# Memory rows and six of sixteen weight pieces loaded into the residual's two row places, and the first weight splits ordered behind the last block of the stage before

## The chip, the cores and the metric

The program runs on one core of a Trainium2 chip. A core has a matrix engine (PE, the trace also names its weight loads PEld), two engines for elementwise work (DVE and ACT), a third slower one (POOL), and SP, which here only issues transfers. The metric is the device time of one execution in microseconds, taken as the median of several runs. Lower is better.

## The reference, cut to what matters

One decoder layer over 1024 tokens of width 1024 in float32: a latent attention and a retention in parallel, one output projection, a cross-attention to 256 memory tokens, and a mixture of 32 gated MLPs. The change lies where the first two meet the third:

```python
x = x + jnp.concatenate([a_out, r_out], axis=-1) @ w_out[l]
hc = rms_norm(x, cross_norm_g[l])
m = rms_norm(mem, mem_norm_g[l])
# memory_cross_attention(hc, m, ...):
q = rms_norm((h @ w_q).reshape(B, S, CROSS_HEADS, CROSS_HEAD_DIM), q_qk_g)
kv = m @ w_kv                       # (256 x 1024) @ (1024 x 2048)
k = rms_norm(kv[..., :D_MODEL].reshape(B, M, CROSS_HEADS, CROSS_HEAD_DIM), k_qk_g)
v = kv[..., D_MODEL:].reshape(B, M, CROSS_HEADS, CROSS_HEAD_DIM)
```

## The kernel before, in words

**Products in three parts.** Every float32 factor is split into a high part (ACT rounds it, `wh`, `oTH`, `mTH`) and a low part (DVE subtracts, `wl`, `oTL`, `mTL`). A product is three matmuls: high by high, high by low, low by high (`mm3`). `split` makes the two parts.

**Weights.** `wpiece` loads two row blocks of a weight matrix (two transfers of 256 KB) into one `raw` place of 512 KB, and splits each block, with the norm's gain multiplied in. `raw` has three places (`RB = 3`), the split pieces have seven (`WB = 7`). `wchunk` makes the four pieces of a column chunk of 512. A `raw` place comes free when both low parts are taken; a split place when the matmuls that read it are done.

**Stages around the change.** Stage C is the latent attention in eight blocks of 128 tokens, with the output projection `out_part` of each block behind it. `out_part(7)`, the last one, needs the transposed attention output `oa` as `oTH` and `oTL`, runs 24 matmuls into `ps_sc`, adds the residual (`xa`, DVE) and squares the sum (ACT, tile names `ps_sc<-xa`). Stage E0 loads the memory rows in two tiles of 128 tokens (512 KB each), takes their squares (ACT, `ckn,sqm<-...`), scales them (DVE) and transposes them on PE into `mTH` and `mTL`. Stage E1 multiplies them with `cross_w_kv`: four column chunks, each with two memory tiles and eight row blocks, 192 matmuls of 128x512 in all. I number the sixteen weight pieces p0 to p15; chunk c uses p(4c) to p(4c+3). Then come the eight pieces of `cross_w_q` (wq0 to wq7) through the same three `raw` places, the first residual rows (`load_x1`, tiles `x1` with two places of 512 KB), their transposes (`x1TH`, `x1TL`), and stage E, the cross-attention. `load_down(0)` also issues one 1 MB load of an expert's weights early in E1.

**What sets the order.** A list scheduler places instructions engine by engine from priorities (`PRI`, `self.at`) and its own costs. At run time each engine executes its list strictly in order; SP likewise issues its transfers in order, and a transfer that has to wait holds up all behind it.

**Before the change**, the two memory tiles took two of the three `raw` places from stage C until PE had transposed them; the first pieces of `cross_w_kv` went through the third place one after the other, and p0 to p2 were split in the middle of stage C.

Of the kernel before, what the change touches and what calls it, by code (L numbers as in the profile page):

```python
# [24 lines left out]
F32 = mybir.dt.float32  # L25
# [4 lines left out]
AF = mybir.ActivationFunctionType  # L30
# [6 lines left out]
D = 1024  # L37
# [68 lines left out]
class Layer:  # L106
    def __init__(self, tc, a, out, dbg=None, stop=None):
        self.tc, self.nc, self.a, self.out, self.dbg, self.stop = tc, tc.nc, a, out, dbg or {}, stop
        self.banks, self.alias, self.place = {}, {}, [1, 2, 3, 4]
        self.ob, self.aT = 1, None  # L110


    def slot(self, shape, dtype=F32, name="t", bufs=2, pool=None, tag=None):
# [36 lines left out]
    def split(self, H, L, src, scale=None):  # L150

        nc = self.nc
        if scale is None:
            nc.scalar.activation(H, src, AF.Copy)  # L154
            return nc.vector.tensor_tensor(L, src, H.bitcast(F32), OP.subtract)
        else:
            self.high = nc.scalar.activation(H, src, AF.Copy, scale=scale)  # L157
            return nc.vector.scalar_tensor_tensor(L, src, scale, H.bitcast(F32), OP.mult, OP.subtract)  # L158

    def transposes(self, dst, src, n):  # L160
# [6 lines left out]
        e = self.mhalf[:, :1].to_broadcast(sh) if len(sh) == 2 else self.mhalf[:, :1, None].to_broadcast(sh)  # L167
        self.nc.gpsimd.tensor_tensor(out, v, e, OP.pow)

    def wpiece(self, srcs, n, gains, name):  # L170

        raw = self.wtile().rearrange("p (k n) -> p k n", k=2)
        pool, bufs = self.W
        if bufs:
            H, L = [pool.tile([128, 2, 512], F32R, name="w" + x, tag="w" + x, bufs=bufs) for x in "hl"]
        else:

            t = pool.tile([128, 2, 2, 512], F32R, name="w", tag="dn%d" % self.place.pop(0), bufs=1)
            H, L = t[:, 0], t[:, 1]
        for i, s in enumerate(srcs):  # L180
            dst = raw[:, i, :n]
            if len(s.shape) == 3:
                dst = dst.rearrange("p (g c) -> p g c", g=s.shape[1])
            self.nc.sync.dma_start(dst, s)
        if gains is None:
            self.split(H[:, :len(srcs), :n], L[:, :len(srcs), :n], raw[:, :len(srcs), :n])
        else:
            for i in range(len(srcs)):
                self.split(H[:, i, :n], L[:, i, :n], raw[:, i, :n], gains[i])
        return [(H[:, i, :n], L[:, i, :n]) for i in range(len(srcs))]  # L190

    def wchunk(self, w, n, gain, nk=8):

        r = []
        for k in range(0, nk, 2):
            ks = [k, k + 1] if k + 1 < nk else [k]
            r += self.wpiece([w(i) for i in ks], n, None if gain is None else [gain[i] if isinstance(gain, list) else gain[:, i:i + 1] for i in ks], "w")
        return r

    def project(self, out, xt, w, part=slice(None)):  # L200
# [585 lines left out]
    def out_part(self, tb, w, ret, role):  # L786

        nc = self.nc
        rows = slice(tb * 128, (tb + 1) * 128)
        if ret is None and tb >= 6:  # L790
            oT = self.split_T(self.oa[tb].rearrange("p h c -> p (h c)"), 4, "oT", self.ob, self.O)
        else:
            m = self.slot([128, 512], name="mr", bufs=self.ob, pool=self.O)
        if ret is not None:
            nc.sync.dma_start(m, ret[rows, :])
            oT = self.to_T(m, 4, "oT", self.ob, role, self.O)
        elif tb < 6:
            nc.sync.dma_start(m.rearrange("v (h t) -> v h t", h=NH),
                              self.mad.rearrange("(h v) t -> v h t", h=NH)[:, :, rows])
            oT = self.split_T(m, 4, "oT", self.ob, self.O)  # L800
        for c in range(2):
            cols = slice(c * 512, (c + 1) * 512)
            xr = self.slot([128, 512], F32, "xr", 1, self.O) if ret is not None else self.slot([128, 512], F32, "xa", XA)
            nc.sync.dma_start(xr, self.a["x"][0][rows, cols] if ret is not None else self.x1d[rows, cols])
            p = self.bank(role)
            self.project(p, oT, w[c])
            nc.vector.tensor_tensor(xr, p, xr, OP.add)
            nc.sync.dma_start(self.x1d[rows, cols], xr)
            if ret is None:
                self.square(self.sx1[:, tb, c:c + 1], xr, p)  # L810
                if "x1" in self.dbg:
                    nc.sync.dma_start(self.dbg["x1"][rows, cols], xr)
# [9 lines left out]
    def phase_e0(self):  # L822

        nc, a, sm = self.nc, self.a, self.sm
        gg = []
        for name in ("cross_q_qk_g", "cross_k_qk_g"):
            g = self.small([128, 2], "g_" + name, bufs=1)
            nc.sync.dma_start(g, a[name][0].rearrange("(k p) -> p k", p=128))
            gg.append(g)
        ggc = sm.tile([128, 2], F32, name="ggc", bufs=1)  # L830
        nc.vector.tensor_tensor(ggc, gg[0], gg[1], OP.mult)
        self.mT = []
        for m in range(2):
            mt = self.wtile("mem")
            nc.sync.dma_start(mt, a["mem"][0][m * 128:(m + 1) * 128, :])
            sq = self.small([128, 4], "sqm")
            for i in range(2):
                self.square(sq[:, i:i + 1], mt[:, i * 512:(i + 1) * 512], self.slot([128, 512], name="ckn", pool=self.CK))
            nc.vector.tensor_tensor(sq[:, 2:3], sq[:, 0:1], sq[:, 1:2], OP.add)
            self.inv_rms(sq[:, 3:4], sq[:, 2:3], D, "rm")  # L840
            self.scaled("mt", mt, mt, sq[:, 3:4])
            self.mT.append(self.to_T(mt, 8, "mT", 4, pool=self.E0))
        self.ggc = ggc

    def phase_e1(self):
        nc, a, mT, ggc = self.nc, self.a, self.mT, self.ggc
        w = a["cross_w_kv"][0]
        self.cK = [[self.slot([128, 2, 256], F32R, "cK", 8, self.KV) for _ in range(2)] for _ in range(NH)]
        self.cV = [[None, None] for _ in range(2)]
        for c in range(4):  # L850
            wc = self.wchunk(lambda k: w[k * 128:(k + 1) * 128, c * 512:(c + 1) * 512], 512, self.gain["mem_norm_g"])
            for m in range(2):
                p = self.bank("pj")
                self.project(p, mT[m], wc)
                if c >= 2:
                    v = [self.slot([128, 512], F32R, "cV" + s, 4, self.KV) for s in "HL"]
                    self.split(*v, p)
                    self.cV[m][c - 2] = v
                    continue
                ph = p.rearrange("p (h c) -> p h c", h=2)  # L860
                st = self.small([128, 2], "stk")
                for h in range(2):
                    self.square(st[:, h:h + 1], ph[:, h], self.slot([128, 256], BF, "jm", 1, self.CK))
                f = self.small([128, 2], "fk")
                self.inv_rms(f, st, 256, "fk")
                kn = self.slot([128, 2, 256], name="ckn", pool=self.CK)
                nc.vector.tensor_tensor(kn, ph, f[:, :, None].to_broadcast([128, 2, 256]), OP.mult)
                with self.at("e1t"):
                    tr = self.bank("tr")
                    self.transposes(tr, kn.rearrange("p h c -> p (h c)"), 4)  # L870
                    for i in range(4):
                        h, d = 2 * c + i // 2, i % 2
                        ms = slice(m * 128, (m + 1) * 128)
                        self.split(self.cK[h][0][:, d, ms], self.cK[h][1][:, d, ms], tr[:, i * 128:(i + 1) * 128],
                                   ggc[:, d:d + 1])
# [826 lines left out]
```

## Time and profile before

| What | Value |
|---|---|
| median of 3 runs | 1211.96 us (1209.45 to 1214.25) |
| the profiled execution | 1214.96 us, of which the span shown is 1213.2 us |
| PE busy | 1162.8 us, 96% of the span |
| DVE, ACT busy | 771.3 us, 652.3 us |
| stages C to E1, roughly | 290 to 530 us, then 530 to 585 us |

All positions are microseconds from the start of the span. A row of the timeline gives start, duration, engine, line, instruction, its output and inputs; in brackets stands the idle time of that engine just before it, and who ended it. Matmul durations overlap: the distance between starts is what a matmul costs (about 0.23 us for 128x512 at full clock). PEclk is the share of full clock that the chip granted: 1.0 is 2.4 GHz, 0.5 is 1.2 GHz.

### The profile page before, as it was taken

The page shows a single profiled execution, that of the slowest core. Times are in us where ns is not written, and L with a number is a line of the kernel's source. Part 1 is how long each engine was busy: PE and PEld are TensorE (multiplying, and loading weights), DVE is VectorE, ACT ScalarE, POOL GpSimd, SP SyncE. Part 2 cuts the span into 40 slices and gives each one's busy share as a digit, 9 for nine tenths or more (in the row PEclk, how much of TensorE's full clock was granted, in tenths as well). Part 3 has the DMA queues.
Part 4 walks back from the last instruction along what each step waited for, and adds up shares of the span by engine and source line. Part 5 has one row for each costly group of instructions (what it writes and reads, how often), then busy time and mean ns, then how long its engine had stood idle before and what let it go on. Part 6 is the DMA issues. An engine that isn't in the chain of part 4 may idle for free. (4 is left out here: it accounts for less than half of the span.)

```text
span 1213.2 us, 18340 instructions
## 1 busy us (share of the span) xinstructions
PE 1162.8 (96%) x6325; PEld 910.7 (75%) x6325; DVE 771.3 (64%) x1938; ACT 652.3 (54%) x1508; POOL 152.0 (13%) x152
## 2 busy tenths in 40 slices
PE   8999999998999999989999999999699999999995
PEld 7887878776688888878899998778565655566552
DVE  5646464678675786658644445555677777777672
ACT  8723232446554664557644446322477777777672
POOL 1011010121100000000000000000222222222222
PEclk9999999999999999999999999999799999999998
DMA  7622020204323433276611024985799999999982
GB/s 237 181 58 80 11 76 10 89 21 132 100 87 104 153 96 120 81 243 191 218 62 62 27 62 150 314 287 210 263 343 343 342 337 334 315 317 315 320 294 45
DMA packets 115472, 213.23 MB, mean 176 GB/s; under 512 B 20577, under 2 KB 68705, under 8 KB 107185
## 3 DMA queue, kind: packets, MB, share of 16 engines
q1 hardware_dynamic: 106912, 194.59, 47.0%
q0 software_dynamic: 7280, 17.37, 6.2%
q8 instruction: 51, 0.84, 0.3%
q14 instruction: 45, 0.36, 0.1%
q10 hardware_dynamic: 1184, 0.07, 0.1%
HBM read 179.69 MB, written 40.11 MB: 181 GB/s over the span
## 5 line engine op out<-in xcount | busy, mean ns | idle before, releaser
L145 PE MATMUL ps_pj<-wh,xT 128*128 128x512 f32 (+1 forms) x640 | 219.9, 403 | 1.8 <-ACT wh L157 1.2
L158 DVE SCALAR_TENSOR_TENSOR L<-raw,g,H 128x512 fp32r<-128x512 f32 x256 | 180.4, 748 | 55.1 <-ACT H L157 52.2
L157 ACT ACTIVATE H<-raw,g 128x512 fp32r<-128x512 f32 x256 | 169.5, 713 | 32.1 <-PE ps_pj L145 22.7
L145 PEld LDWEIGHTS ps_pj<-wh,xT 128*128 128x128 f32 x640 | 121.1, 190 | 21.1 <-ACT wh L157 1.6
L145 PE MATMUL ps_pj<-wl,xT 128*128 128x512 f32 (+1 forms) x320 | 127.9, 400 | 0.0
L1500 PE MATMUL ps_sc<-raw,aT 128*96 128x512 f32 x256 | 117.6, 602 | 1.2 <-ACT aT L1484 1.0
L145 PE MATMUL ps_pj<-H,xH 128*96 128x512 f32 x256 | 116.2, 454 | 0.0
L145 PE MATMUL ps_pj<-L,xH 128*96 128x512 f32 x256 | 102.6, 401 | 0.1
L145 PE MATMUL ps_pj<-H,xL 128*96 128x512 f32 x256 | 102.0, 398 | 0.0
L1500 PEld LDWEIGHTS ps_sc<-raw,aT 128*96 128x96 f32 x256 | 39.1, 162 | 65.1 <-issue 51.1
L1492 POOL DMA_INDIRECT out_dram<-y,idx x31 | 54.4, 1756 | 201.4 <-ACT H L157 161.6
L145 PE MATMUL ps_pj<-x1TH,wh 128*128 128x256 f32 x256 | 74.3, 290 | 2.6 <-ACT x1TH L154 2.6
L145 PE MATMUL ps_pj<-x1TL,wh 128*128 128x256 f32 x256 | 75.2, 294 | 0.0
L145 PE MATMUL ps_pj<-x1TH,wl 128*128 128x256 f32 x256 | 74.4, 291 | 0.0
L145 PEld LDWEIGHTS ps_pj<-wl,xT 128*128 128x128 f32 x320 | 61.1, 191 | 8.5 <-DVE wl L158 0.5
L145 PEld LDWEIGHTS ps_pj<-H,xH 128*96 128x96 f32 x256 | 42.5, 166 | 22.3 <-issue 7.5
L459 ACT ACTIVATE tg<-ps_pj,rh 128x128 f32<-128x128 f32 x32 | 11.7, 366 | 87.7 <-PE ps_pj L145 87.6
L145 PEld LDWEIGHTS ps_pj<-L,xH 128*96 128x96 f32 x256 | 41.7, 163 | 22.4 <-DVE L L158 8.6
L145 PEld LDWEIGHTS ps_pj<-H,xL 128*96 128x96 f32 x256 | 41.5, 162 | 16.0 <-issue 0.7
L145 PEld LDWEIGHTS ps_pj<-x1TH,wh 128*128 128x128 f32 x256 | 48.4, 189 | 3.0 <-ACT x1TH L154 3.0
L1030 ACT ACTIVATE cP<-ps_sc,cnb,fcq 128x256 f32<-128x256 f32 x32 | 17.8, 561 | 57.9 <-DVE cnb L1025 57.9
L145 PEld LDWEIGHTS ps_pj<-x1TH,wl 128*128 128x128 f32 x256 | 48.6, 190 | 0.0
(412 smaller groups left out, 2882.3 us busy)
## 6 DMA issues: line engine op xcount, KB each, us to landing
raw<-in_expert_w_down_dram SPq DMA_DIRECT2D x32, 1024.0 KB
raw<-in_expert_w_gate_dram SPq DMA_DIRECT2D x32, 1024.0 KB
raw<-in_expert_w_up_dram SPq DMA_DIRECT2D x32, 1024.0 KB
raw<-in_w_in_dram SPq DMA_DIRECT2D x32, 256.0 KB
raw<-in_cross_w_kv_dram SPq DMA_DIRECT2D x32, 256.0 KB
x<-x1d SPq DMA_DIRECT2D x16, 512.0 KB
xr<-in_x_dram SPq DMA_DIRECT2D x16, 256.0 KB
raw<-in_w_out_dram SPq DMA_DIRECT2D x16, 256.0 KB
```

Of the source, the lines that this page charges most:

```text
L145: mm = lambda s, m, i, e: self.nc.tensor.matmul(out, s, m, start=i, stop=e, skip_group_check=skip)
L157: self.high = nc.scalar.activation(H, src, AF.Copy, scale=scale)
L158: return nc.vector.scalar_tensor_tensor(L, src, scale, H.bitcast(F32), OP.mult, OP.subtract)
L459: nc.scalar.activation(tg, p[:, 384:512], AF.Tanh, scale=rh[:, tb:tb + 1])
L1030: nc.scalar.activation(P[:, js], s[:, js], AF.Exp, bias=nb[:, j:j + 1], scale=f[:, j:j + 1], accum_out=su[:, j:j + 1])
L1492: add = lambda c, cs: sums.append(nc.gpsimd.indirect_dma_start(out=out, out_offset=bass.IndirectOffsetOnAxis(ap=rows[:, c:c + 1], axis=0), ...
L1500: nc.tensor.matmul(py[:CAP], act[:, j * CAP:(j + 1) * CAP], wd[:, j, cs], start=(j == 0), stop=(j == 1))
```

## The change

It has three parts. The memory tiles are loaded into the two `x1` places. Pieces 1, 3, 6, 8, 11 and 13 of `cross_w_kv` are loaded into the `x1` places too, the other ten into `raw`. The high parts of the first chunk's pieces are ordered, for the scheduler, behind the high part of the last block's `oT` (`self.last`); the wait is one of order alone, with no semaphore of its own.

```diff
     def split(self, H, L, src, scale=None):
         if scale is None:
-            nc.scalar.activation(H, src, AF.Copy)
+            self.high = nc.scalar.activation(H, src, AF.Copy)
             return nc.vector.tensor_tensor(L, src, H.bitcast(F32), OP.subtract)
         else:
             self.high = nc.scalar.activation(H, src, AF.Copy, scale=scale)
+            if self.first:
+                self.after(self.high, self.first, "rows of the stage before first")
...
-    def wpiece(self, srcs, n, gains, name):
+    def wpiece(self, srcs, n, gains, name, raw=None):
-        raw = self.wtile().rearrange("p (k n) -> p k n", k=2)
+        raw = (self.wtile() if raw is None else raw).rearrange("p (k n) -> p k n", k=2)
...
     def out_part(self, tb, w, ret, role):
             oT = self.split_T(self.oa[tb].rearrange("p h c -> p (h c)"), 4, "oT", self.ob, self.O)
+            self.last = self.high
...
     def phase_e0(self):
-            mt = self.wtile("mem")
+            mt = self.slot([128, D], F32, "x1", 2, self.X1)
...
     def phase_e1(self):
+        raw = lambda i: self.slot([128, D], F32, "x1", 2, self.X1) if i % 5 in (1, 3) else None
         for c in range(4):
-            wc = self.wchunk(lambda k: w[k * 128:(k + 1) * 128, c * 512:(c + 1) * 512], 512, self.gain["mem_norm_g"])
+            self.first = None if c else self.last
+            wc = self.wchunk(lambda k: w[k * 128:(k + 1) * 128, c * 512:(c + 1) * 512], 512, self.gain["mem_norm_g"],
+                             raw=lambda i: raw(4 * c + i))
```

Three places in the lists show what moves. First ACT at the end of stage C, before the change; `mem_6104` and `mem_6134` are the memory tiles, `oTH_6027` is the last block's transposed output, `wh_6200` are the high parts of p3 and `wh_6307` those of p4:

```order
L731 ACTIVATE oa_5942<-ps_po_5824 128x512
L348 ACTIVATE ckn_6107,sqm_6106<-mem_6104 128x512
L348 ACTIVATE ckn_6109,sqm_6106<-mem_6104 128x512
L348 ACTIVATE ckn_6137,sqm_6136<-mem_6134 128x512
L348 ACTIVATE ps_sc_5993,sx1_3381<-xa_5991 128x512
L348 ACTIVATE ckn_6139,sqm_6136<-mem_6134 128x512
L154 ACTIVATE oTH_6027<-oa_5942 128x512
L348 ACTIVATE ps_sc_6011,sx1_3381<-xa_6009 128x512
L157 ACTIVATE wh_6200<-raw_6199,mem_norm_g_351 128x512 x2
L348 ACTIVATE ps_sc_6033,sx1_3381<-xa_6031 128x512
L348 ACTIVATE ps_sc_6051,sx1_3381<-xa_6049 128x512
L157 ACTIVATE wh_6307<-raw_6306,mem_norm_g_351 128x512
```

The same place after the change, where the memory tiles are `x1_6104` and `x1_6134` and `wh_6173` are the high parts of p0:

```order
L734 ACTIVATE oa_5942<-ps_po_5824 128x512
L351 ACTIVATE ps_sc_5993,sx1_3381<-xa_5991 128x512
L351 ACTIVATE ckn_6107,sqm_6106<-x1_6104 128x512
L351 ACTIVATE ckn_6109,sqm_6106<-x1_6104 128x512
L351 ACTIVATE ps_sc_6011,sx1_3381<-xa_6009 128x512
L154 ACTIVATE oTH_6027<-oa_5942 128x512
L157 ACTIVATE wh_6173<-raw_6172,mem_norm_g_351 128x512 x2
L351 ACTIVATE ckn_6137,sqm_6136<-x1_6134 128x512
L351 ACTIVATE ckn_6139,sqm_6136<-x1_6134 128x512
L351 ACTIVATE ps_sc_6033,sx1_3381<-xa_6031 128x512
L351 ACTIVATE ps_sc_6051,sx1_3381<-xa_6049 128x512
L154 ACTIVATE mTH_6121<-ps_tr_6116 128x512
```

`oTH_6027` now stands behind the second square of the residual (`ps_sc_6011`), and `mTH_6121` directly behind the last one, with no weight split between. Second, SP's list at the same place, before the change (`raw_6306` is p4, `raw_6315` p5, `raw_6808` the expert's 1 MB):

```order
L888 DMA x1_6630<-x1d_60 128x1024
L808 DMA x1d_60<-xa_6009 128x512
L804 DMA xa_6031<-x1d_60 128x512
L804 DMA xa_6049<-x1d_60 128x512
L184 DMA raw_6306<-in_cross_w_kv_dram 128x512
L808 DMA x1d_60<-xa_6031 128x512
L184 DMA raw_6306<-in_cross_w_kv_dram 128x512
L808 DMA x1d_60<-xa_6049 128x512
L184 DMA raw_6315<-in_cross_w_kv_dram 128x512 x2
L1411 DMA raw_6808<-in_expert_w_down_dram 128x2x1024
L184 DMA raw_6324<-in_cross_w_kv_dram 128x512 x2
```

And after it (`x1_6181` is p1, `x1_6199` p3, `x1_6324` p6; p0, p2 and p4 are issued in stage C, before these rows):

```order
L839 DMA x1_6134<-in_mem_dram 128x1024
L812 DMA x1d_60<-xa_6009 128x512
L808 DMA xa_6031<-x1d_60 128x512
L808 DMA xa_6049<-x1d_60 128x512
L186 DMA raw_6315<-in_cross_w_kv_dram 128x512 x2
L812 DMA x1d_60<-xa_6031 128x512
L812 DMA x1d_60<-xa_6049 128x512
L186 DMA x1_6181<-in_cross_w_kv_dram 128x512 x2
L1419 DMA raw_6808<-in_expert_w_down_dram 128x2x1024
L186 DMA x1_6199<-in_cross_w_kv_dram 128x512 x2
L186 DMA x1_6324<-in_cross_w_kv_dram 128x512 x2
```

The second memory tile stands where the second residual tile was loaded, p1 behind the last write of the residual, and p3 behind the 1 MB load. The residual rows themselves are now loaded between the last pieces of `cross_w_kv` and the first of `cross_w_q`. On PE the matmuls of chunk 0 are the same 48, but those of the two memory tiles alternate, where before the first tile's 24 stood ahead of the second's.

## Rows read from the trace of the kernel before

**Rows 1.** The page: busy share of each engine over the span.
```profile
PE 1162.8 (96%) x6325; PEld 910.7 (75%) x6325; DVE 771.3 (64%) x1938; ACT 652.3 (54%) x1508; POOL 152.0 (13%) x152
```
**Rows 2.** Timeline of PE, lines with a wait, and two starts beside them.
```profile
524.74 0.50 PE L145 MATMUL ps_sc<-wh,oTH 128*128 128x512 f32 x1 [0.61 <-ACT oTH L154]
...
530.32 1.03 PE L162 MATMUL ps_tr<-ident,mem 128*128 128x128 f32 x8
533.75 0.50 PE L145 MATMUL ps_pj<-wh,mTH 128*128 128x512 f32 x1 [2.40 <-ACT mTH L154]
...
547.89 0.60 PE L162 MATMUL ps_tr<-ident,ckn 128*128 128x128 f32 x4
...
586.93 0.58 PE L145 MATMUL ps_pj<-x1TH,wh 128*128 128x256 f32 x1 [2.59 <-ACT x1TH L154]
```
**Rows 3.** Windows: length, busy time (instructions) of PE, PEld, DVE, ACT, POOL, PEclk, DMA share, GB/s.
```profile
440.00:460.00 20.00, 20.00 (x112) 17.02 (x112) 15.27 (x38) 12.52 (x35) 1.01 (x1) 1.00 0.60 190
...
535.00:540.00 5.00, 5.00 (x20) 4.21 (x19) 3.57 (x6) 2.42 (x4) 0.00 (x0) 0.66 0.93 306
540.00:584.00 44.00, 44.00 (x203) 35.37 (x201) 32.27 (x61) 31.42 (x69) 2.80 (x4) 1.00 0.65 209
584.00:590.00 6.00, 3.41 (x16) 2.95 (x15) 4.21 (x8) 4.15 (x8) 0.00 (x0) 0.72 0.49 159
236.00:240.00 4.00, 2.48 (x13) 1.72 (x12) 2.29 (x9) 1.09 (x5) 1.02 (x1) 1.00 0.23 82
```
**Rows 4.** Timeline of PE: the longest wait inside the window 236 to 240.
```profile
238.40 0.33 PE L162 MATMUL ps_trp<-ident,kn 128*128 128x128 f32 x1 [1.52 <-DVE kn L608]
```
**Rows 5.** Tile `raw`, 400 to 525 us: duration min/median/max, first and last start.
```profile
L157 ACT ACTIVATE wh<-raw,mem_norm_g x6: 710/726/739, 436.8 to 453.1; 128x512 fp32r<-128x512 f32 x6
L158 DVE SCALAR_TENSOR_TENSOR wl<-raw,mem_norm_g,wh x6: 746/750/755, 437.6 to 453.8; 128x512 fp32r<-128x512 f32 x6
```
**Rows 6.** Timeline of ACT and DVE around the last output block.
```profile
524.07 0.62 ACT L154 ACTIVATE oTH<-oa 128x512 fp32r<-128x512 f32 x1
524.19 0.69 DVE L807 TENSOR_TENSOR xa<-ps_sc,xa 128x512 f32<-128x512 f32 x1
524.91 0.60 ACT L348 ACTIVATE ps_sc<-xa 128x512 f32<-128x512 f32 x1 [0.22 <-DVE xa L807]
...
531.30 0.60 ACT L348 ACTIVATE ps_sc<-xa 128x512 f32<-128x512 f32 x1 [0.88 <-DVE xa L807]
532.50 0.72 ACT L157 ACTIVATE wh<-raw,mem_norm_g 128x512 fp32r<-128x512 f32 x1 [0.47 <-DMA raw<-in_cross_w_kv_dram]
533.12 1.07 ACT L154 ACTIVATE mTH<-ps_tr 128x512 fp32r<-128x512 f32 x2
```
**Rows 7.** Timeline of SP's issues at the end of stage C.
```profile
517.79 0.42 SPq L888 DMA_DIRECT2D x<-x1d  x1
...
529.09 0.33 SPq L184 DMA_DIRECT2D raw<-in_cross_w_kv_dram  x1
...
531.23 0.32 SPq L808 DMA_DIRECT2D x1d<-xa  x1
...
534.93 0.38 SPq L1411 DMA_DIRECT2D raw<-in_expert_w_down_dram  x1
```
**Rows 8.** The end of E1: SP, DVE and ACT.
```profile
564.89 0.74 DVE L158 SCALAR_TENSOR_TENSOR wl<-raw,mem_norm_g,wh 128x512 fp32r<-128x512 f32 x1
565.70 0.80 SPq L184 DMA_DIRECT2D raw<-in_cross_w_q_dram  x2
570.28 0.72 ACT L157 ACTIVATE wh<-raw,cross_norm_g 128x512 fp32r<-128x512 f32 x1 [2.00 <-DMA raw<-in_cross_w_q_dram]
571.16 1.32 ACT L157 ACTIVATE wh<-raw,mem_norm_g 128x512 fp32r<-128x512 f32 x2
573.40 0.80 SPq L184 DMA_DIRECT2D raw<-in_cross_w_q_dram  x2
585.81 1.06 ACT L154 ACTIVATE x1TH<-ps_tr 128x512 fp32r<-128x512 f32 x2
```

More of the change, by code (lines that the diff above doesn't have):

```diff
@@ L109, in __init__ @@
         self.banks, self.alias, self.place = {}, {}, [1, 2, 3, 4]
-        self.ob, self.aT = 1, None
+        self.ob, self.aT, self.first = 1, None, None
     def slot(self, shape, dtype=F32, name="t", bufs=2, pool=None, tag=None):
@@ L190, in wpiece, with wchunk @@
         return [(H[:, i, :n], L[:, i, :n]) for i in range(len(srcs))]
-    def wchunk(self, w, n, gain, nk=8):
+    def wchunk(self, w, n, gain, nk=8, raw=lambda i: None):
         r = []
@@ L196, in wchunk @@
             ks = [k, k + 1] if k + 1 < nk else [k]
-            r += self.wpiece([w(i) for i in ks], n, None if gain is None else [gain[i] if isinstance(gain, list) else gain[:, i:i + 1] for i in ks], "w")
+            r += self.wpiece([w(i) for i in ks], n, None if gain is None else [gain[i] if isinstance(gain, list) else gain[:, i:i + 1] for i in ks], "w",
+                             raw(k // 2))
         return r
```

## The prediction

> **What bounds the kernel now.** I read the page's busy times first: PE is busy 96% of the span [rows 1]. So a change that touches no matmul can only gain where PE waits, or where it runs at half clock. Next I read PE's timeline around the change for its waits. There are three: 0.61 us for `oTH` of the last output block, 2.40 us for `mTH`, the transposed memory rows, and 2.59 us for `x1TH` at the end of E1 [rows 2]. Then the windows, for the clock: behind the second wait the granted clock is 0.66 over 5 us with PE fully busy, which loses 5 x 0.34 = 1.7 us; behind the third it is 0.72 over 6 us, 1.7 us, of which some falls on idle time: PE was busy 3.41 of the 6 us, and from the restart at 586.93 nearly all of the rest, so I count 1.3 us [rows 3]. Between them, 540 to 584, PE is full at full clock [rows 3]. All there is to gain at this place is thus 0.6 + 2.4 + 1.7 + 2.6 + 1.3 = 8.6 us. Not every wait costs clock: after 1.52 us at 238.40 [rows 4] the window still shows 1.00 [rows 3].
>
> **Stage C.** Six splits leave it: 6 x 0.73 us of ACT and 6 x 0.75 us of DVE, between 436.8 and 453.8 [rows 5]. PE shows no wait in 440 to 460 [rows 3], so the work given back is hidden, and I take 0.3 us of gain. But the scheduler also reorders PE's list around the folded output weights. The same instructions stand there in another order; nothing in the rows prices that, and I bound it by the waits of this size that the neighbourhood shows, four or five of 0.6: 3 us either way.
>
> **The last output block.** Before, ACT makes `oTH` at 524.07, ahead of the second residual square at 524.91; that square waits for DVE's sum, which starts at 524.19 when PE is done [rows 6]. In the new list `oTH` stands behind it, so it starts at 524.91 + 0.6 = 525.5: 1.45 us later, and PE's wait grows from 0.61 to 2.06 us. The memory tile that two squares ahead of it now wait for is issued where the first residual tile was, 517.79 [rows 7]; a landing of up to 4.6 us (below) puts it at 522.4, early enough. A wait of 2.06 us lies between 1.52 (clock kept) and 2.40 (clock lost), and nearer to the latter. I take it as kept, because 24 matmuls follow it without a gap, and give the other side its own price, 1.7 us.
>
> **The memory rows.** PE's 24 matmuls and eight transposes then end 1.45 us later. Before, ACT had a weight split between the last residual square (531.30) and `mTH` (533.12), held by a transfer [rows 6]; now `mTH` follows the square directly: 531.30 + 0.6 + 1.45 plus DVE's hand-over, about 533.35, so PE starts E1 at 534.0 instead of 533.75. That is +0.25 us. PE's wait there shrinks from 2.40 to about 1.15 us, below the 1.52 that kept the clock: -1.7 us.
>
> **The first chunk.** Before, p0 to p3 were split or ready. Now only p0 is split, p2 and p4 are loaded, and p1 and p3 cannot be issued until PE has transposed the tiles whose places they take. What a 256 KB load needs: the one issued at 529.09 [rows 7] let ACT go on at 532.50 [rows 6], 3.4 us; the one of 565.70 at 570.28 [rows 8], 4.6 us. p1 is queued on SP behind the last write of the residual, 531.23 before [rows 7] and 532.7 now, so it is issued at 533.1, lands at 536.5 to 537.7 and is split 0.72 us later. PE, alternating the two tiles, wants it at about 537.0 (nine matmuls and eight transposes after 534.0): a wait of 0.2 to 1.4 us, taken as 0.8. p3 is queued behind the 1 MB load, which waits for the write of the residual to land: 534.93 - 531.23 = 3.7 us [rows 7], so 536.4 now, and p3 at 536.8. One MB at the 306 GB/s of [rows 3] is 3.4 us. If p3 waits behind all of it, it lands at 543.2 to 544.4, otherwise at 540.2 to 541.4; PE wants its split at 543.0. A wait of 0 to 2.1 us, taken as 0.8. The Trainium skill (DMA: Bandwidth & Descriptors, Queues, rings and completion order) says that each DMA engine consumes the descriptors of its ring in order, which speaks for the late end and against the change; its fixed cost of about 2.0 us plus the bytes (Anatomy of one DMA) would estimate 2.6 us for p1's load, and no wait for p1. The rows' 3.4 and 4.6 us are longer, and I stay with them.
> Chunk 0 ended at 547.89 [rows 2]; now at 547.9 + 0.25 - 1.7 + 0.8 + 0.8 = 548.05. From there PE has no gap, as before; with five places the later loads run further ahead.
>
> **The end of E1.** `x1TH` waits on ACT behind the last splits of `cross_w_q`, whose loads run through the three `raw` places. One of them holds p15, loaded long before its split place is free; before, p15's split also stood behind a wait of 2.00 us for wq1 and came at 571.16, and wq3 could only be issued at 573.40 [rows 8]. Now p13 sits in an `x1` place, so wq0 takes p12's place, two splits (1.5 us) earlier, and p14's second low split, 564.89 [rows 8], stands one small instruction (0.3 us) earlier, which issues wq1 at 565.4. With wq0 out of its way wq1 needs 3.4 to 4.6 us: the chain to `x1TH` is 0.3 to 1.5 us earlier, taken as 1.0. Two residual tiles (1 MB) are put into this queue; they are needed by the transposes near 574, and wait for p11 and p13 only. The wait of 2.59 becomes 1.6 us: -1.0. At 1.6, next to the 1.52 that kept it, the clock holds: -1.3.
>
> **The sum.** Stage C -0.3, `oTH` and `mTH` +0.25, clock -1.7, loads +1.6, end of E1 -1.0, clock -1.3: -2.45 us. Against the profiled execution that is 1214.96 - 2.45 = 1212.5. That execution lies 3.0 above the median of the runs shown, so I forecast 1209.5. I assume that the later stages pass it on whole: their lists are unchanged. If loads rather than PE set the time there, part is lost, at worst all.
>
> **The rivals.** *A, the clock falls at the output block.* The 2.06 us are nearer to 2.40 than to 1.52. Then the 24 matmuls lose 1.7 us and all behind is that much later: -0.75, or 1211. *B, the loads run well ahead.* If five places bring wq7 in 2.6 us sooner, the third wait goes too: another 1.6; with stalls of 0.2 and 0 in chunk 0 (1.4 better) the sum is -5.5, and a stage C better by 1 makes -6.5: 1205.5. For it: PE has no wait in 540 to 584. Against it: p15 still blocks one place. *C, slower: p3 comes late.* From p3 landing after 546 on, PE stands more than 2.4 us in chunk 0, behind p1's 1.4. Loads +4.4 instead of +1.6, the first fall of clock +1.7 as in A and a second in chunk 0 +1.7, the end of E1 no better (+2.3 against my sum): with the stage C term the sum is -2.45 + 2.8 + 1.7 + 1.7 + 2.3 = +6: 1218. Half of that is 1215. For it: three of chunk 0's four pieces used to be split early, and one MB stands ahead of p3. Against it: the alternating order gives PE 30 matmuls ahead of p3. *D, it doesn't do what it says:* the reordered stage C costs more than E1 gains, up to +3 - 2.1 = about +1: 1213.
>
> **How the numbers follow.** A change of 0.5% (6.1 us: below 1205.9 or above 1218.0) is about what a measurement of this kernel can tell from none. Chances: forecast 0.42 (1207 to 1212), A 0.20, B 0.17, C 0.13, D 0.08. Beyond 0.5%: most of B (0.13) and, with a doubled stage C error, 0.01 of the rest for faster, half of C (0.06) and 0.01 of D for slower; so faster 0.14, same 0.79, slower 0.07. The range leaves out the far halves of B and C: 1204.5 to 1215.5, which also takes in stage C's 3 us.
>
> **What would show it.** In the new profile: PE's wait for `oTH` near 2.1 us, that for `mTH` near 1.2 with clock 1.00 in 535 to 540; waits for `wh` of p1 and p3 under 2 us together, near 537 and 543; that for `x1TH` near 1.6 with clock 1.00 behind it. Wrong it is if the clock falls behind `oTH` (A), if `x1TH` is not waited for (B), if one wait in chunk 0 exceeds 2.4 us (C), or if stage C's end moves by more than 1 us (D).

## The result, and the profile after

The changed kernel takes 1219.15 us (median of 8 runs, 1215.93 to 1220.85), the kernel before, timed beside it, 1213.08 (8 runs, 1209.45 to 1215.98). The ratio is 1.0054, with a 95% interval of 1.0038 to 1.0070: slower by some 6.5 us, where 2.45 us less were forecast. The profiled execution took 1218.76 us (span 1216.9).

PE's timeline after the change follows; the first and the last line are marks, the others are waits (length and releaser stand in brackets). They answer to [rows 2].

```profile
414.11 0.61 PE L164 MATMUL ps_tr<-ident,P 128*128 128x128 f32 x4
...
429.80 0.39 PE L145 MATMUL ps_sc<-kv,qTH 128*128 128x256 f32 x1 [0.51 <-ACT P L701]
434.77 0.50 PE L145 MATMUL ps_fl<-wh,oTH 128*128 128x512 f32 x1 [0.84 <-DVE wl L155]
...
526.69 0.50 PE L145 MATMUL ps_sc<-wh,oTH 128*128 128x512 f32 x1 [2.06 <-ACT oTH L154]
...
534.53 0.50 PE L145 MATMUL ps_pj<-wh,mTH 128*128 128x512 f32 x1 [1.15 <-ACT mTH L154]
538.45 0.50 PE L145 MATMUL ps_pj<-wh,mTH 128*128 128x512 f32 x1 [0.46 <-ACT wh L157]
544.67 0.50 PE L145 MATMUL ps_pj<-wh,mTH 128*128 128x512 f32 x1 [1.04 <-ACT wh L157]
551.14 0.33 PE L164 MATMUL ps_tr<-ident,ckn 128*128 128x128 f32 x1 [1.91 <-DVE ckn L875]
592.05 0.58 PE L145 MATMUL ps_pj<-x1TH,wh 128*128 128x256 f32 x1 [4.41 <-ACT x1TH L154]
...
603.07 0.28 PE L145 MATMUL ps_sc<-cK,qTH 128*128 128x256 f32 x1
```

The same two marks on PE before:

```profile
414.37 0.60 PE L162 MATMUL ps_tr<-ident,P 128*128 128x128 f32 x4
...
596.65 0.28 PE L145 MATMUL ps_sc<-cK,qTH 128*128 128x256 f32 x1
```

Ahead of the first mark the two traces differ by 0.26 us in favour of the changed kernel, behind the last by 6.42 against it. So 6.7 us are lost between them, about what the medians say; of this the profiled execution gives 2.7 back in later stages, which I did not follow up. The forecast waits are there almost to the digit: oTH 2.06, mTH 1.15, p1 and p3 together 1.50 (forecast 1.6). New are 1.91 us for `ckn`, the first normalised keys, and x1TH at 4.41 instead of 1.6.

The windows of the changed kernel answer to [rows 3] (PEclk is the third number from the end): the clock behind mTH is kept, as forecast, and at the end of E1 it is at its lower level for longer than before.

```profile
535.00:540.00 5.00, 4.54 (x24) 3.37 (x23) 3.73 (x7) 3.52 (x6) 0.00 (x0) 1.00 0.77 231
...
590.00:594.00 4.00, 1.95 (x8) 1.82 (x9) 3.25 (x5) 2.50 (x5) 0.00 (x0) 0.64 0.26 98
594.00:598.00 4.00, 4.00 (x21) 4.00 (x20) 2.61 (x3) 1.82 (x3) 0.00 (x0) 0.50 0.80 270
```

What stands ahead of ckn is read from the queues of SP and ACT, and then from PE's list. SP's issues: the 1 MB of the expert, then p3; later a residual row, then wq1.

```profile
535.71 0.38 SPq L1419 DMA_DIRECT2D raw<-in_expert_w_down_dram  x1
536.62 0.33 SPq L186 DMA_DIRECT2D x<-in_cross_w_kv_dram  x1
...
566.21 0.33 SPq L896 DMA_DIRECT2D x<-x1d  x1
569.03 0.33 SPq L186 DMA_DIRECT2D raw<-in_cross_w_q_dram  x1
```

ACT's list, in its order:

```profile
543.89 0.72 ACT L157 ACTIVATE wh<-x,mem_norm_g 128x512 fp32r<-128x512 f32 x1 [3.65 <-DMA x<-in_cross_w_kv_dram]
...
547.63 0.39 ACT L351 ACTIVATE jm<-ps_pj 128x256 bf16<-128x256 f32 x1
548.00 0.71 ACT L157 ACTIVATE wh<-x,mem_norm_g 128x512 fp32r<-128x512 f32 x1
548.62 0.37 ACT L351 ACTIVATE jm<-ps_pj 128x256 bf16<-128x256 f32 x1
...
574.55 0.73 ACT L157 ACTIVATE wh<-raw,cross_norm_g 128x512 fp32r<-128x512 f32 x1 [3.40 <-DMA raw<-in_cross_w_q_dram]
...
575.43 0.71 ACT L157 ACTIVATE wh<-raw,mem_norm_g 128x512 fp32r<-128x512 f32 x1
```

p3 lets ACT go on 7.3 us after its issue (536.62 to 543.89). ACT runs its list in order: it idles 3.65 us for p3, then six splits, four of them of p4 and p5, run ahead of the first key square `jm` at 547.63, and one of p6 between the squares. Before, ACT made the first square at 542.50.

Yet the square does not start later than PE lets it. PE ends the products of the first memory tile at 547.61 (its signal in the trace), 0.02 us before the square starts; before, the signal came at 542.47, as close ahead of it. What changed is how much work PE has left from there to the transposes. Square, root and scaling (`ckn` on DVE) and the work behind the tile, before:

```profile
542.50 0.38 ACT L348 ACTIVATE jm<-ps_pj 128x256 bf16<-128x256 f32 x1 [4.13 <-PE ps_pj L145]
545.27 0.69 DVE L867 TENSOR_TENSOR ckn<-ps_pj,fk 128x512 f32<-128x512 f32 x1 [0.82 <-POOL fk L168]
...
542.30 0.39 PE L145 MATMUL ps_pj<-wh,mTH 128*128 128x512 f32 x1
...
547.66 0.39 PE L145 MATMUL ps_pj<-wh,mTL 128*128 128x512 f32 x1
```

and after:

```profile
550.39 0.69 DVE L875 TENSOR_TENSOR ckn<-ps_pj,fk 128x512 f32<-128x512 f32 x1 [0.82 <-POOL fk L170]
...
547.43 0.40 PE L145 MATMUL ps_pj<-wh,mTL 128*128 128x512 f32 x1
...
548.84 0.40 PE L145 MATMUL ps_pj<-wh,mTL 128*128 128x512 f32 x1
```

From the first square to the end of `ckn` it takes 3.5 us in both. Before, 24 matmuls (5.4 us) stand behind the first tile and hide it; with the tiles alternating, 7 (1.6 us) do, and PE waits the difference, 1.9 us.

At the end of E1 a split does stand behind another's load: p15's (575.43, before 571.16 in [rows 8]) comes behind wq1's, which waits for its load.

### The profile page after: what moved, and what is told of

Its sections match the earlier page's. It is cut to its first block, busy times and chain, and to the rows that moved or that the text cites. A ratio compares the mean times of both kernels' runs of the same rounds, so it can differ in the third digit from the quotient of the medians.

```text
span 1216.9 us, 18337 instructions
## 1 busy us (share of the span) xinstructions
PE 1161.2 (95%) x6325; PEld 909.5 (75%) x6325; DVE 770.7 (63%) x1938; ACT 652.1 (54%) x1508; POOL 156.9 (13%) x152
## 5 line engine op out<-in xcount | busy, mean ns | idle before, releaser
L1500 POOL DMA_INDIRECT out_dram<-y,idx x31 | 58.7, 1893 | 199.1 <-ACT H L157 175.9
L145 PEld LDWEIGHTS ps_pj<-x1TL,wh 128*128 128x128 f32 x256 | 49.2, 192 | 0.0
```

The source lines that it names most:

```text
L145: mm = lambda s, m, i, e: self.nc.tensor.matmul(out, s, m, start=i, stop=e, skip_group_check=skip)
L1500: add = lambda c, cs: sums.append(nc.gpsimd.indirect_dma_start(out=out, out_offset=bass.IndirectOffsetOnAxis(ap=rows[:, c:c + 1], axis=0), ...
```

## The experiments

Each is timed over five rounds beside the kernel before, on one chip; e1 to e4, e5 to e8, e9 to e12 and e13 to e15 ran on four different chips, so across these groups only ratios are compared. Ratios are to the kernel before (the changed kernel: 1.0054). Waits are PE's in the profiled execution, in us; a dash stands for less than 0.4. A profile is one execution and can lie 5 us from its kernel's median (e5), so I go by waits more than by positions.

| run | ratio (95%) | oTH | mTH | p1 / p3 | ckn | x1TH |
|---|---|---|---|---|---|---|
| before | 1 | 0.6 | 2.4 | - | - | 2.6 |
| after | 1.0054 (1.0038-1.0070) | 2.1 | 1.2 | 0.5 / 1.0 | 1.9 | 4.4 |
| e1 expert load behind p3 | 1.0011 (0.9997-1.0026) | 2.1 | 1.2 | 0.6 / - | - | 1.9 |
| e2 places for p1, p3 only | 1.0065 (1.0049-1.0081) | 2.1 | 1.2 | 0.4 / 0.6 | 1.9 | 4.7 |
| e3 places for p6 to p13 only | 1.0039 (1.0025-1.0054) | 2.1 | 3.3 | - | - | 2.0 |
| e4 memory rows only | 1.0015 (1.0001-1.0029) | 2.1 | 1.2 | - | - | 3.1 |
| e5 no hold | 1.0036 (1.0021-1.0051) | 2.1 | 1.2 | 0.4 / 0.9 | 1.9 | 3.9 |
| e6 oTH ahead | 1.0040 (1.0024-1.0056) | 0.6 | 1.5 | 0.8 / - | 1.9 | 2.5 |
| e7 = e1 + e6 | 1.0002 (0.9986-1.0018) | 0.6 | 1.5 | 0.9 / - | - | 2.2 |
| e8 = e4 + e6 | 1.0022 (1.0008-1.0035) | 0.6 | 3.5 | - | - | - |
| e9 squares ahead | 1.0077 (1.0052-1.0103) | 2.1 | 1.2 | - / 0.8 | 1.1 | 5.0 |
| e10 = e7, larger loads | 1.0027 (1.0012-1.0041) | 0.6 | 1.4 | 0.8 / 1.0 | - | 2.4 |
| e11 = e10, p1 raw | 1.0028 (1.0013-1.0043) | 0.6 | 2.4 | - | - | 2.9 |
| e12 = e7, places as e2 | 1.0030 (1.0013-1.0046) | 0.6 | 1.5 | 0.9 / - | - | 4.4 |
| e13 chunk 0 raw, held | 1.0021 (1.0008-1.0034) | 0.6 | 1.4 | - | 3.2 | 3.7 |
| e14 places at the end | 1.0024 (1.0010-1.0039) | 0.6 | 1.4 | - | 1.7 | 3.0 |
| e15 only p12 to p15 | 1.0025 (1.0011-1.0039) | 0.6 | 1.3 | - | 2.0 | 2.4 |

**The load ahead of p3 (e1).**

```diff
+            if k == 6 and self.first:
+                self.p3 = self.load
...
         self.wd.append(self.ring("dn", n))
-        self.expert_weight(self.wd[n], 2, ORDER[n])
+        d = self.expert_weight(self.wd[n], 2, ORDER[n])
+        if n == 0:
+            self.after(d, self.p3, "keys' fourth piece first")
```

> The 1 MB load of the first expert's down weights is queued behind both loads of p3 instead of ahead of them; nothing else is moved by hand. Theory 1 (in chunk 0, p3's late landing holds ACT's list, so the key squares and the first keys come late, and the 3.3 us go on to the end of E1): p3 is issued near 536, lands near 540 to 541 instead of 543.9, PE's waits of 1.04 us for its split and of 1.9 us for the first ckn go, chunk 0 ends near 548, x1TH is some 3 us earlier, and the whole is 2.5 to 3.5 us faster than the changed kernel (0.997 of it). Rival 1 (ACT's list of eight weight splits ahead of the squares costs the 1.9 us whenever p3 lands): the 1.0 us for p3 goes, the ckn wait stays near 1.9, gain 1.0. Rival 2 (the loss is made at the end of E1 by the residual rows in the queue of the query weights): PE's wait for x1TH grows by what chunk 0 gains, and the time stays.

In e1 SP issues p3's loads, the first at 539.15, and then the expert's:

```profile
539.15 0.33 SPq L186 DMA_DIRECT2D x<-in_cross_w_kv_dram  x1
540.12 0.38 SPq L1421 DMA_DIRECT2D raw<-in_expert_w_down_dram  x1
```

ACT waits 0.48 us in place of 3.65 (the split of p3's second half):

```profile
543.91 0.73 ACT L157 ACTIVATE wh<-x,mem_norm_g 128x512 fp32r<-128x512 f32 x1 [0.48 <-DMA x<-in_cross_w_kv_dram]
```

PE's waits for p3 and ckn are gone, and its last wait shrinks to 1.90:

```profile
588.57 0.38 PE L145 MATMUL ps_pj<-x1TH,wh 128*128 128x256 f32 x1 [1.90 <-ACT x1TH L154]
```

This one edit takes 0.0043 off the ratio, some 5 us and more than theory 1 asked for: four fifths of the loss. But the scheduler built new lists around the moved load, so the 5 us are not the load's place alone. On PE 15 matmuls stand behind the first tile's last product (signal at 546.91) in place of 7, on ACT no split stands between the first two squares, and wq3 is issued earlier (574.18 instead of 577.68). The wait for p3 goes with the load's place; that for ckn goes with these lists as well, and no run holds them apart.

**The squares (e9).** The splits of p5 to p7 held behind chunk 0's squares:

```diff
+        self.sq = self.nc.scalar.activation(out, src, AF.Square, accum_out=acc)
...
-        raw = lambda i: self.slot(...) if i % 5 in (1, 3) else None
+        def raw(i):
+            if i == 5:
+                self.first = self.sq
+            return self.slot(...) if i % 5 in (1, 3) else None
```

> The changed kernel, with the splits of p5, p6 and p7 held behind the four key squares of chunk 0 on ACT; loads, places and expert load stay, so p3 is as late as before. Theory 1 (the ckn wait of 1.91 us comes from ACT's order: behind the late p3 stand splits of the next chunk ahead of the squares): the wait for p3 stays near 1.0, that for ckn falls below 0.8, chunk 0 ends 1 to 1.9 us earlier, and the whole is 1 to 2 us faster than the changed kernel. Rival 7 (the squares are late because PE itself ends the projections late, behind p3): the ckn wait stays above 1.5 and nothing is gained.

ACT in e9 has the square free, but it now waits for PE:

```profile
548.33 0.38 ACT L351 ACTIVATE jm<-ps_pj 128x256 bf16<-128x256 f32 x1 [1.16 <-PE ps_pj L145]
```

PE in e9:

```profile
551.07 0.33 PE L164 MATMUL ps_tr<-ident,ckn 128*128 128x128 f32 x1 [1.14 <-DVE ckn L878]
...
592.71 0.58 PE L145 MATMUL ps_pj<-x1TH,wh 128*128 128x256 f32 x1 [5.03 <-ACT x1TH L154]
```

The ckn wait falls by 0.8: that much was ACT's order, a split of p6 between the first two squares. The other 1.1 is not ACT's: the first square now waits for PE, which has the same 7 matmuls left behind it. So theory 1 and rival 7 are both half right, and neither half grows with p3's lateness: the wait for ckn is 1.9 in the changed kernel, e2, e5 and e6, where PE waits 1.0, 0.6, 0.9 and 0.3 us for p3. Nothing is gained: the new list makes wq0's issue late (569.55 instead of 564.56), and the wait for x1TH takes it all.

**oTH ahead (e6), and both edits (e7).** The last block's split gets a priority 400 higher:

```diff
+            self.tc.cur_priority -= 400 * (tb == 7)
             oT = self.split_T(self.oa[tb]..., 4, "oT", self.ob, self.O)
+            self.tc.cur_priority += 400 * (tb == 7)
```

> The changed kernel with the last output block's split oTH put one residual square and one memory square further ahead on ACT; the load order stays. Theory 2 (the wait of 2.06 us for oTH costs itself and, in most executions, the clock behind it, though the profile of the changed kernel showed it kept): the wait falls to about 0.4 us, the granted clock stays 1.00 through 520 to 535, E1 starts 1.6 us earlier on the engine's own time, and the whole is 2 to 3 us faster than the changed kernel. Rival 6 (the delay is swallowed by p1 and p3, which come from the transposed memory rows and from the residual's last write): waits in chunk 0 grow by what oTH gives, and the gain is under 0.7 us.

> Both edits: oTH ahead, and the first expert's load behind p3. If the two losses are separate, the gains add up: 4.2 us of the first run's edit and 2 to 3 of oTH, that is 6 to 7 us faster than the changed kernel, 0 to 1 us faster than the kernel before (ratio 0.999). If the end of E1 is bound by the query weights' loads, PE's wait for x1TH grows from 1.9 by what oTH gives, and the sum is 4 to 5 us, at or above the kernel before.

PE in e6:

```profile
526.28 0.50 PE L145 MATMUL ps_sc<-wh,oTH 128*128 128x512 f32 x1 [0.55 <-ACT oTH L154]
...
589.64 0.38 PE L145 MATMUL ps_pj<-x1TH,wh 128*128 128x256 f32 x1 [2.48 <-ACT x1TH L154]
```

e6 is 1.7 us faster than the changed kernel by the ratios (0.0014), less than the 2 to 3 expected, and with overlapping intervals, so the gain is not settled. With e1's edit the two roughly add up (0.0043 + 0.0014 against 0.0052): e7 stands where the kernel before stands, not below it.

**The parts alone (e3, e4, e5, e8).** e4 moves only the memory rows (weights all through raw places, no hold); e8 is e4 with e6's edit; e5 drops only the hold; e3 leaves x1 places to p6, p8, p11 and p13:

```diff
-            self.first = None if c else self.last      # e4, e5, e8
+            self.first = None
-        ... if i % 5 in (1, 3) else None                # e4, e8: False; e3: i in (6, 8, 11, 13)
```

> Only the memory rows are moved to the x1 places: all weights of keys and values go through the raw places and nothing is held behind the last output block, so stage C has its six splits again. Theory 1: the wait for mTH falls to about 1.2 us and the clock behind it is kept as in the changed kernel, oTH is still late (2.1 us), chunk 0 has no wait, the residual rows come ahead of the query weights as soon as the memory rows are transposed, and the end of E1 is as before or earlier: 1 to 3 us faster than the kernel before, 7 to 9 faster than the changed one. Rival 4 (the moved memory rows themselves cost, by the late oTH and by residual rows in the queue of the weights): not faster than the kernel before.

> Only the memory rows in x1 places, no weights there and no hold, and oTH ahead as in the run before it. Theory 2: the wait for oTH falls from 2.06 to about 0.4 and the clock stays; gain of 2 us on the kernel with the memory rows alone, so 0.9995 of the kernel before. Against the run with both edits it tells what the weights' places are worth: if they bring the query weights earlier, as I had forecast, it is 0.5 to 1 us slower than that one; if not, it is as fast.

> The changed kernel without the hold: the first pieces' splits may again stand in stage C; the places of memory rows and weights stay. Theory 1 (p1 and p3 are late because of their places and the expert load ahead of p3): only p0 and what is loaded early can be split there, p1 and p3 come as late as before, PE's waits for p3 and ckn stay near 1.0 and 1.9, and the time is that of the changed kernel within 1 us (1.005 of the kernel before). Rival 5 (the hold is the loss, since three of the four pieces of chunk 0 used to be split early): 3 us or more faster than the changed kernel.

> p1 and p3 go through the raw places, p6, p8, p11 and p13 stay in x1 places; the splits of the first chunk still stand behind the last output block. Theory 1: p1 is loaded in stage C and p3 is issued when p0's split frees its place (about 532), ahead of the expert load, so chunk 0 has no wait above 0.5 us and ends near 547.5 to 548; 3 us of the loss go. The end of E1 keeps the residual rows in the queue: x1TH waits about 3 to 4 us. Sum about 3 us faster than the changed kernel, as the kernel before or up to 1 us above it. Rival 2: gain of 1 us or less, with a wait for x1TH of over 5 us.

e4 refutes my view that the memory rows alone are a gain: 1.0015, as rival 4 has it. With oTH ahead (e8) it is no better, because weight splits, the last of them waiting 0.52 us for its load, now stand ahead of mTH on ACT: 3.54 us. The same happens in e3 (3.29). The hold alone is not the loss: without it the waits of chunk 0 are the same, and the times' intervals overlap.

**The places for later weights (e2, e12).**

```diff
-        ... if i % 5 in (1, 3) else None
+        ... if i in (1, 3) else None     # e2: on the changed kernel; e12: on e7
```

> Only p1 and p3 go to x1 places; p6, p8, p11 and p13 go through the three raw places, so the residual rows' two 512 KB loads no longer wait for p11 and p13. Theory 1: chunk 0 stays as slow as in the changed kernel (waits for p3 about 1.0 and for ckn about 1.9), the query weights' loads have no residual rows ahead, wq1 lands 4.6 us after its issue instead of 5.5, PE's wait for x1TH is near 3.4 instead of 4.4, gain 1.0 us or a little more. Rival 2 (the residual rows make the loss): the wait for x1TH falls to 2.6 or less and the gain is 3 us or more. Rival 3 (five places do help, as I had forecast): without the places the wait grows above 4.4 and the time is 1 us worse than the changed kernel.

> As the run with both edits, but only p1 and p3 in x1 places, the rest through raw. It tells what the x1 places for p6 to p13 are worth when chunk 0 is not late. My forecast's step (wq0 is issued earlier with them, x1TH 1.0 us earlier): the wait for x1TH is 1 us longer here than the 2.23 of the run with both edits, and the time 1 to 2 us longer. Theory 4 (the gain is given back, since the residual rows then lie in the queue of the query weights): wait and time are the same within 0.5 us.

e2 is not faster, so the residual rows in the queue are not the loss. e12 against e7 prices the places once chunk 0 is in time. The last wait of e7, then of e12:

```profile
586.64 0.39 PE L145 MATMUL ps_pj<-x1TH,wh 128*128 128x256 f32 x1 [2.23 <-ACT x1TH L154]
```

```profile
588.09 0.58 PE L145 MATMUL ps_pj<-x1TH,wh 128*128 128x256 f32 x1 [4.40 <-ACT x1TH L154]
```

2.2 us of wait, and 0.0028 of the ratio (3.4 us, with intervals that just overlap): the step of the forecast that five places bring the query weights earlier (wq0 is issued at 561.19 in e7, 565.12 in e12) is right, and was hidden by chunk 0.

**Stage C and p1 (e10, e11).** One 512 KB DMA for each piece of chunk 0, by which PE's order up to 436 us is the old one; e11 also gives p1 a raw place:

```diff
+            self.load = self.nc.sync.dma_start(raw, whole)   # rows k and k+1 of the piece in one
-        ... if i % 5 in (1, 3) else None                       # e11
+        ... if i in (3, 6, 8, 11, 13) else None
```

> As the run with both edits (oTH ahead, expert load behind p3), and each piece of chunk 0 is loaded by one 512 KB DMA instead of two of 256 KB, by which PE's order in stage C up to 436 us is that of the kernel before again. Theory 3 (stage C's reordering, which I had put at -0.3 us, costs 1.0 to 1.3 us by the two waits of 0.51 and 0.84 us for qTH and oTH at 430 to 436): both waits go, stage C is 1.0 to 1.3 us shorter, and the whole is about 1 us faster than the run with both edits, 0.999 of the kernel before. Rival: the larger loads make p1 or p3 later by 0.5 us or more, and nothing is left of it.

> As the run before it, with p1 in a raw place (loaded in stage C) and p3, p6, p8, p11, p13 in the x1 places. Theory 1: PE's wait for p1 (0.85 us in the run with both edits) goes, p3 is issued as soon as the memory rows are transposed and is there in time; 0.5 to 1 us faster than the run before it, near 0.998 of the kernel before. Rival: splits of p1 and p2 stand ahead of mTH on ACT, mTH comes later, and the gain is lost, as where all of chunk 0 went through raw places (3.29 us for mTH).

The two waits at 430 and 435 go, but stage C is no shorter: from 415 to 521 us PE loses 1.04 us against the kernel before in e10, 1.00 in e7. The edit brings a wait of its own, though: the 512 KB load now stands ahead of a residual row in SP's list, DVE waits 1.03 us for that row (0.31 before), and PE waits for DVE (1.65 us in e11):

```profile
419.87 0.50 PE L145 MATMUL ps_fl<-wh 128*128 128x512 f32 x1 [0.56 <-DVE xr L820]
```

So e10 neither shows theory 3 nor refutes it, and what stage C's loss hangs on stays open. The larger loads make p3 late (1.0 us); in e11 mTH takes up what p1 gives.

**The end of E1 (e13 to e15).** On e7: splits from p1 on held behind the last mTH, and x1 places for p6, p8, p11, p13 (e13), for p6, p8, p12 to p15 (e14), for p12 to p15 (e15):

```diff
+        self.mTlast = self.high
...
+            if i == 1:
+                self.first = self.mTlast
-        ... if i % 5 in (1, 3) else None
+        ... if i in (6, 8, 12, 13, 14, 15) else None     # e14
```

> As the run with oTH ahead and the expert load behind p3; chunk 0 goes through raw places (p0 to p2 loaded in stage C), p6, p8, p11 and p13 through x1 places, and the splits from p1 on are held behind the last mTH. Theory 1 (only loads that come late, and ACT's order around them, cost time in chunk 0): PE's waits for p1 and p3 and for ckn are all below 0.4 us, that for mTH is near 1.5, chunk 0 ends 0.8 us earlier than in the run with both edits; x1TH waits 2 to 3 us; the time is that of the kernel before or up to 1 us less (0.999 to 1.000). Rival: p3, issued when p0's split frees its place, lands late; p3 or ckn is waited for by 1 us or more.

> As the run before it, but the x1 places hold p6, p8 and p12 to p15, so that the first three pieces of the query weights find raw places without waiting for p13 to p15. Theory 5 (the wait for x1TH is the chain of query weights, 22 to 26 us from wq0's issue to x1TH in all kernels so far, so only an earlier wq0 shortens it): wq0 is issued 3 us or more earlier, near 558, x1TH's wait falls below 0.5 us and the clock behind it is kept: 3 to 4 us faster than the kernel before (0.997). Rival 8: the residual rows, now behind p14 and p15, come late, and x1TH waits for them 2 us or more; no gain.

> As the run before it, but only p12 to p15 in x1 places. Theory 5: wq0 is again issued early; with p6 and p8 in raw places it is some 0 to 3 us later than in the run before it, and x1TH's wait 0 to 1.5 us; 0.997 to 0.999 of the kernel before. Rival 8 as there.

In e13 no weight of chunk 0 is late for PE, and still ckn is, by more than ever. ACT in e13:

```profile
545.84 0.72 ACT L157 ACTIVATE wh<-raw,mem_norm_g 128x512 fp32r<-128x512 f32 x1 [5.43 <-DMA raw<-in_cross_w_kv_dram]
546.47 0.36 ACT L353 ACTIVATE jm<-ps_pj 128x256 bf16<-128x256 f32 x1
```

PE in e13:

```profile
549.96 0.33 PE L164 MATMUL ps_tr<-ident,ckn 128*128 128x128 f32 x1 [3.18 <-DVE ckn L883]
```

Here it is ACT's list that does it: a split of the next chunk, which PE does not need yet, waits 5.43 us for its load, and the square behind it, for which PE was done at 542.60, starts 3.9 us later, the moment the split is done. In the changed kernel the stall of 3.65 us held the square no longer than PE's own products did. In e14 wq0 is issued 5.8 us earlier than in the changed kernel, but SP's list then stops at the residual rows, which wait for the places of p14 and p15; wq4 comes only behind them:

```profile
558.74 0.33 SPq L186 DMA_DIRECT2D raw<-in_cross_w_q_dram  x1
...
571.93 0.33 SPq L904 DMA_DIRECT2D x<-x1d  x1
574.88 0.33 SPq L904 DMA_DIRECT2D x<-x1d  x1
576.82 0.33 SPq L186 DMA_DIRECT2D raw<-in_cross_w_q_dram  x1
```

So theory 5 (wq0's issue sets x1TH) falls. Rival 8 names the right rows: PE waits for them itself by 0.85 us in e14 and by 1.06 and 0.86 in e15, and x1TH then waits for the query weights behind them. No version beat the kernel before; e7 and, within the noise, e1 equal it.

## Why the prediction was wrong, point by point

The forecast's terms against the profile, between the two marks above: stage C -0.3, measured +0.8; oTH and mTH +0.25, measured +0.3; chunk 0 (clock -1.7, loads +1.6) -0.1, measured +2.5; the wait for x1TH -1.0, measured +1.8; the clock behind it -1.3, measured +1.3. Together -2.45 and +6.7.

- **The first chunk** is the step that failed. The prediction closes it with "From there PE has no gap, as before" and so puts the wait for the chunk's keys at nothing, without a reason. Its other terms were right in size: p3 came at 543.89 (forecast 543.2 to 544.4, the late end), and the two waits are 1.50 us for 1.6. It had the alternating tiles in view, but only for the time that they win ahead of p1 and p3. They also leave 7 matmuls (1.6 us) in place of 24 (5.4 us) behind the first tile, while its squares, root and scaling take 3.5 us: 1.91 us of new wait for ckn. e9 shows that 0.8 of it hangs on a split between two squares; with 15 matmuls and adjacent squares (e1, e7, e12) it is gone. That PE's order makes the other 1.1 is read from the traces; no run changed that order alone. Of the chunk's +2.5, about 0.9 is left when the waits and the kept clock are taken off, and I do not account for it. My rival C had the direction, and nearly the time, but not the cause: p3 did not land after 546, and no wait in chunk 0 passed 2.4 us.
- **p1's load** let ACT go on 4.0 us after its issue (533.69 to 537.67), inside the rows' 3.4 to 4.6. The prediction's 2.6 us, which it takes from the Trainium skill (DMA: Bandwidth & Descriptors, Anatomy of one DMA), go by a fit which that page gives for transfers issued by GpSimd; these are issued by SP.
- **The end of E1** was forecast 1.0 earlier and came 5.1 later. Its working (wq0 two splits earlier) holds: e12 against e7. What failed is that it took chunk 0 as in time. Of the 5.1, 3.3 is the delay with which chunk 0 ends, handed on (0.8 of it from the stages ahead); the other 1.8 is wq1, which let ACT go on 5.5 us after its issue where I had counted with 3.4 to 4.6, and p15's split and wq3 behind it. In e1 and e6 wq1 took 3.4 and 3.6 us, so part of the 1.8 is the spread of one load. The clock term had the wrong sign for the same reason: a longer wait, and a longer stretch at the lower level.
- **The last output block.** 2.06 us as forecast, and the clock held in this execution. That I took it as kept was luck: see the last section. The reason I gave, 24 matmuls behind the wait without a gap, does not decide it, since the same 24 stand there in the executions where the clock fell. e6 takes the wait away for a gain of about 1.7 us, which its interval does not settle.
- **Stage C** was mis-sized by 1.1 us, and no run says why.
- **The memory rows** came out as worked: 1.15 us, and full clock in 535 to 540.

## What to carry to other kernels

When a change reorders an engine's list, ask two things of each result, and not only whether its operands come in time. How much work does the engine have left between the result's end and the first use of what others make from it? Here 24 matmuls behind the first tile became 7, and a chain of 3.5 us that had been hidden cost 1.9. And what stands behind an instruction that waits for a load, in the list of its own engine? In e13 a split that nobody needed yet held a square back by 3.9 us, and PE waited 3.18. Then look at what is queued ahead of an urgent load: here 1 MB for the experts, which PE first reads at 884 us in the trace of before. And an edit that moves one load also moves the scheduler's lists, so compare the lists before you credit the load.

## What the runs showed of the hardware that was not expected

Whether a wait costs clock is not settled by its length around 2 us. The wait for oTH is 2.06 us in seven profiled executions. The clock granted in 520 to 530 and 530 to 540 us stayed at full speed in two (the changed kernel and e5) and fell in five (e1, e2, e3, e4, e9), as in this window of e2 (0.83):

```profile
520.00:530.00 10.00, 7.94 (x28) 5.93 (x27) 5.35 (x11) 5.70 (x16) 1.12 (x2) 0.83 0.64 214
```

In all nine executions where the wait was 0.55 or 0.56 us it was 1.00 in 520 to 530. For x1TH, a wait of 1.90 us was followed by 0.68 in 590 to 594 (e1), one of 2.44 us by full clock (e10). A forecast should carry such a term with a chance, not as kept or lost.

A 256 KB load, for which the rows of before gave 3.4 to 4.6 us, let ACT go on 7.3 us after its issue (p3, 536.62 to 543.89) when 1 MB had been issued 0.9 us ahead of it on the same queue. The Trainium skill (DMA: Bandwidth & Descriptors, Queues, rings and completion order) says that each DMA engine takes the descriptors of its ring in order; the 7.3 us agree with it.
